# Sigmoid gates rewritten as tanh with VectorE products, and the low weight halves of the input projection moved to VectorE

## The chip, the cores and the metric

The kernel runs on one core of a Trainium2 chip. The metric is the device time of one execution in microseconds; the median of the runs shown stands for the kernel. Five engines work side by side: TensorE (PE in the profile, with its weight loads as PEld), VectorE (DVE), ScalarE (ACT), GpSimd (POOL) and SyncE (SP), which issues the DMAs here. Each engine runs its own instructions strictly in order.

## The reference

Two layers of a hybrid block over 1024 tokens of width 1024, in float32. Cut to what matters here:

```python
h = rmsnorm(x, norm_mix[l])
proj = h @ w_in[l]                      # q | k | v | u | ug | ga | gb : 34 column tiles of 128
a_out = sliding_window_attention(q, k, v, sinks[l])      # window 128, 16 heads, QK norm, rotary
c_out = conformer_conv(u, ug, ...)      # a = u * sigmoid(ug); causal depthwise conv, width 31;
                                        # layernorm; silu; pointwise
merged = sigmoid(ga) * a_out + sigmoid(gb) * c_out
x = x + merged @ w_out[l]
x = x + swiglu(rmsnorm(x, norm_ffn[l]))
```

## The kernel before

Activations lie transposed, channels on the 128 partitions and the 1024 tokens along the row, so a tile is 128x1024. Each matmul of float32 data is made of three matmuls on halves (`mm3`, L236): a value is cut into a high part of type fp32r and a low part, the rest, and high·high, high·low and low·high are added up in PSUM. For the weights, `fetch` (L120) loads one column tile of 128 output channels (`raw`, 128x1024, 512 KB, two buffers) by a DMA on SP, ACT casts it to the high part `wh` (L133, three buffers), and POOL subtracts to get the low part `wl` (L134, two buffers).

A layer is a mix stage (input projection, attention, convolution, merge) and a feed-forward stage. The work of the mix stage is one long loop over 34 projection tiles in the order INPROJ: key and value first, then 30 tiles, then two at the end. `dense` (L257) makes one tile in eight steps of six matmuls and counts a clock step (`tick`, L227) after each. All that goes on beside the projections is hung on this clock: `after(n, fn)` puts `fn` n steps ahead, and what it issues then stands at that place among PE's matmuls. PE's order is written out in this way for the whole program, DVE's for the mix stage only (L755 to the end of the loop). ACT, POOL and SP are ordered by the scheduler of the framework.

Beside the projections run:

- 32 attention units (`unit_s`, L625), one every six steps. Scores S by PE; a copy to SBUF by ACT; mask, maximum `mx` and `nm` by DVE (`top`, 2.2 steps later); the exponentials by ACT (L656), the reciprocal `ri` of their sum by DVE (`norm`, T2 = 3.5 steps after S, L661), scaling by ACT (L663); transposes `pT` by PE (7.5 steps after S); high and low parts `ph` (ACT) and `pl` (DVE, L679); four masks by POOL (L684, L687, tiles `mo`, `ph`, `pl`); the product with the values into `po` by PE (L702), which waits for these masks; and the addition into `A` by DVE (L714).
- Eight query tiles (`queries`, L581), each with a rotation: four DMAs `rot<-q` on SP, two products on POOL (L385, L386), the power that makes the norm (`fq`, L396, POOL), and on DVE a sum (L400) and a low part (L610).
- The convolution (`conv_taps`, L485): per channel tile a first tap (L492) and 30 more (L496) on DVE, one every 1.42 steps, four tiles in a row. Its input `a` is u·sigmoid(ug): ACT's Sigmoid and a product on POOL (L482). After each tile POOL adds it to `lsum` (L502).
- The gates (`gate`, L722): DVE scales the projection (L724), ACT takes Sigmoid (L725). For `ga` a product with A follows on POOL (`mul_a`, L735) and a DMA; `gb` goes to DRAM and is multiplied later (L811).

Reciprocals, taps and low parts thus share one DVE queue whose order is fixed. ACT keeps one set of function tables at a time, and loads another (`ACT_TABLE_LOAD`) wherever Exp and Sigmoid alternate.

Of the kernel before, what the change touches and what calls it, by code (L numbers as in the profile page):

```python
# [12 lines left out]
F32 = mybir.dt.float32  # L13
F32R = mybir.dt.float32r
U32 = mybir.dt.uint32
AF = mybir.ActivationFunctionType
ALU = mybir.AluOpType
# [12 lines left out]
CC = 4  # L30
CW = 31
# [13 lines left out]
V_CWT = 30  # L45
# [7 lines left out]
def trunk(ctx, tc, xT, win, wcv, wout, wgu, wdn, vecs, cosT, sinT, outT):  # L53
    nc = tc.nc
# [61 lines left out]
        wends.append(len(wseq))  # L116
    raws, ready, given = [], [], [0, 0, 0]
    part = [0]

    def fetch(limit=len(wseq)):  # L120
        limit = min(limit, wends[part[0]])
        while given[2] < limit and given[2] <= given[0] + AHEAD + 1:
            src, n = wseq[given[2]]
            raw = wp.tile([P, n], F32, tag="raw", bufs=WRAW, name="raw")
            nc.sync.dma_start(raw, src)
            raws.append(raw)
            given[2] += 1
        while given[1] < given[2] and given[1] <= given[0] + AHEAD:
            n = wseq[given[1]][1]
            raw = raws.pop(0)  # L130
            wh = wp.tile([P, n], F32R, tag="wh", bufs=WHI, name="wh")
            wl = wp.tile([P, n], F32R, tag="wl", bufs=WLO, name="wl")
            nc.scalar.copy(wh, raw)  # L133
            nc.gpsimd.tensor_tensor(out=wl, in0=raw, in1=wh.bitcast(F32), op=ALU.subtract)  # L134
            ready.append((wh, wl))
            given[1] += 1

    def next_w():
        fetch()
        given[0] += 1  # L140
        return ready.pop(0)
# [68 lines left out]
    def at(when, fn):  # L210
        heapq.heappush(events, (when, next(serial), fn))

    def after(n, fn):
        at(clock[0] + n, fn)
# [52 lines left out]
    def t4(name):  # L267
        return tp.tile([P, T], F32, tag="t4", bufs=T4, name=name)
# [52 lines left out]
    for l in range(DEPTH):  # L321
# [32 lines left out]
        ct = mp.tile([P, T], F32, name="ct")  # L354
        st_ = mp.tile([P, T], F32, name="st_")
# [11 lines left out]
        rot = ap_.tile([P, T], F32, name="rot")  # L367
# [9 lines left out]
        def inproj():  # L377
            return dense(xs)

        def rope(src):  # L380
            for h in range(2):
                o = h * HD
                nc.sync.dma_start(rot[o:o + 8], src[o + 8:o + 16])
                nc.sync.dma_start(rot[o + 8:o + 16], src[o:o + 8])
            nc.gpsimd.tensor_tensor(out=src, in0=src, in1=ct, op=ALU.mult)  # L385
            nc.gpsimd.tensor_tensor(out=rot, in0=rot, in1=st_, op=ALU.mult)  # L386

        def headnorm(sq, f):
            pss = ps_o("pssh")
# [78 lines left out]
        held_u = {}  # L468
        avals = {}
# [6 lines left out]
        def conv_g(c, ps):  # L476
            ug = t4("ug")
            nc.vector.tensor_tensor(out=ug, in0=ps, in1=R, op=ALU.mult)
            nc.scalar.activation(ug, ug, AF.Sigmoid)
            a = ap_.tile([P, T + CW - 1], F32, tag="a", bufs=2, name="a")  # L480
            nc.gpsimd.memset(a[:, 0:CW - 1], 0.0)
            nc.gpsimd.tensor_tensor(out=a[:, CW - 1:], in0=held_u.pop(c), in1=ug, op=ALU.mult)  # L482
            after(6, lambda: avals.update({c: a}))

        def conv_taps():  # L485
            for c in range(CC):
                while c not in avals:
                    yield 0
                a = avals.pop(c)
                w0 = V_CWT + c * CW  # L490
                y = ap_.tile([P, T], F32, tag="y", bufs=1, name="y")
                nc.vector.tensor_scalar(out=y, in0=a[:, 0:T], scalar1=V(w0), scalar2=V(V_CB + c),  # L492
                                        op0=ALU.mult, op1=ALU.add)
                yield 1
                for j in range(1, CW):
                    nc.vector.scalar_tensor_tensor(out=y, in0=a[:, j:j + T], scalar=V(w0 + j),  # L496
                                                   in1=y, op0=ALU.mult, op1=ALU.add)
                    if j == CW - 1:
                        if c == 0:
                            nc.scalar.copy(lsum, y)  # L500
                        else:
                            nc.gpsimd.tensor_tensor(out=lsum, in0=lsum, in1=y, op=ALU.add)  # L502
                        nc.sync.dma_start(yd[c], y)
                    yield 1
            while True:
                yield 0

        taps = conv_taps()
        conv_done = [0]

# [70 lines left out]
        def queries(i, ps):  # L581
            q32 = t4("q32")
            nc.scalar.activation(q32, ps, AF.Copy, scale=V(V_GQ))
            sq = t4("sqh")
            nc.scalar.activation(sq, ps, AF.Square)
            rope(q32)
            fq = sm.tile([P, 16], F32, tag="fq", bufs=3, name="fq")
            nfq = sm.tile([P, 16], F32, tag="nfq", bufs=3, name="nfq")
            sr = sm.tile([P, NB, 2], F32, tag="sr", bufs=3, name="sr")
# [33 lines left out]
        Av = {}  # L623
# [98 lines left out]
        def gate(ps):  # L722
            g = t4("g")
            nc.vector.tensor_tensor(out=g, in0=ps, in1=R, op=ALU.mult)  # L724
            nc.scalar.activation(g, g, AF.Sigmoid)  # L725
            return g

        done_o = set()
# [1 line left out]
        def mul_a(i):  # L730
            if (i, 3) not in done_o:
                after(1, lambda: mul_a(i))
                return
            g = gheld.pop(i)
            nc.gpsimd.tensor_tensor(out=g, in0=g, in1=Av.pop(i), op=ALU.mult)  # L735
            nc.sync.dma_start(mA[i], g)


# [14 lines left out]
        after(0 if l else NA, norm_a)  # L753
        dve = ExitStack()
        dve.enter_context(tc.manual_schedule(engines={mybir.EngineType.DVE}))  # L755
        keys(psk)
        tick()
        def project(j):
# [24 lines left out]
        while events:  # L783
            tick()
        assert conv_done[0] == CC * CW
        dve.close()
        att.close()

# [16 lines left out]
        for i in range(8):  # L805
            ga = zp.tile([P, T], F32, tag="ga", bufs=3, name="ga")
            nc.sync.dma_start(ga, mA[i])
            gb = zp.tile([P, T], F32, tag="gb", bufs=3, name="gb")
            nc.sync.dma_start(gb, sB[i])
            ps = dense(zs, True)  # L810
            nc.vector.tensor_tensor(out=gb, in0=ps, in1=gb, op=ALU.mult)  # L811
            nc.vector.tensor_tensor(out=gb, in0=gb, in1=ga, op=ALU.add)
            ms.append(split_plain(gb, f"m{i}"))
        zp_s.close()
# [8 lines left out]
        xacc = [xp.tile([P, T], F32, name=f"xa{e}") for e in range(KD)]  # L823
# [4 lines left out]
        for e in range(KD):  # L828
            nc.sync.dma_start(xacc[e], xT[e] if l == 0 else xnx[e])
            ps = dense(ms, True)  # L830
            if e >= KD - 3:
                ahead(2 * (e - KD + 4))
            nc.vector.tensor_tensor(out=xacc[e], in0=xacc[e], in1=ps, op=ALU.add)
            nc.sync.dma_start(xsp[e], xacc[e])
            tick()
        rgt.close()
# [28 lines left out]
        for e in range(KD):  # L865
            x, g = xacc[e], V(V_GF + e)
            for n in range(2):
# [4 lines left out]
                                               op0=ALU.mult, op1=ALU.subtract)  # L872
# [80 lines left out]
        for f in FORD[:NCL]:  # L953
# [4 lines left out]
            for m in range(2):  # L958
                bs = [bank(), bank()]
                held.append(bs)  # L960
                for kk in range(2):
                    a = next_p()
# [19 lines left out]
        for i, f in enumerate(FORD):  # L982
# [6 lines left out]
            g, u = t4("g"), t4("u")  # L989
# [105 lines left out]
        for n, (name, _, _) in enumerate(DOWN):  # L1095
# [3 lines left out]
            for p in range(NG - fl):  # L1099
                w, a = next_p(), next_p()  # L1100
                for e in range(4):
                    prod(bs[e], w, e, a[0], a[1], go and p == 0, False)
                if 1 <= p < 5 and name in HALVES:
                    up, n = HALVES[name]
# [41 lines left out]
S0 = 16  # L1146
SP = 6.0
TAIL = 2
T1, T2, SCB = 2.2, 3.5, 2
QSP = 7  # L1150
TS = 1.42
LN1 = 7
# [4 lines left out]
QN = 5  # L1157
QSB = 4
WRAW, WHI, WLO, T4 = 2, 3, 2, 4


def _tables():
# [60 lines left out]
```

## Time and profile before

| | us |
|---|---|
| runs shown | 2695.49, 2704.43, 2702.65 |
| median | 2702.65 |
| the profiled execution | 2704.77 |
| its span, first to last instruction | 2703.0 |

| engine | busy us | share of the span |
|---|---|---|
| PE | 2588.6 | 96% |
| DVE | 1843.6 | 68% |
| POOL | 1601.5 | 59% |
| ACT | 1190.6 | 44% |

The page's share of PE counts its pipelined matmuls at their modelled length, so 96% does not say that PE is at its peak; where the granted clock of TensorE is under 1.00, a matmul takes longer and is still busy time. The shares are means over stages that differ: in the mix stage, roughly 105 to 560 us and again 1445 to 1900 us, DVE and POOL work much harder than in the rest. Times are given from the start of the span. In a row of a timeline the columns are start, duration, engine, line, operation, tiles (written <- read), shapes and count, and in brackets how long the engine stood idle just before and what ended that. A row of a group adds up many instructions: busy time and mean duration stand behind the bar.

### The profile page before, as it was taken

The page shows a single profiled execution, that of the slowest core. Times are in us where ns is not written, and L with a number is a line of the kernel's source. Part 1 is how long each engine was busy: PE and PEld are TensorE (multiplying, and loading weights), DVE is VectorE, ACT ScalarE, POOL GpSimd, SP SyncE. Part 2 cuts the span into 40 slices and gives each one's busy share as a digit, 9 for nine tenths or more (in the row PEclk, how much of TensorE's full clock was granted, in tenths as well). Part 3 has the DMA queues.
Part 4 walks back from the last instruction along what each step waited for, and adds up shares of the span by engine and source line. Part 5 has one row for each costly group of instructions (what it writes and reads, how often), then busy time and mean ns, then how long its engine had stood idle before and what let it go on. Part 6 is the DMA issues. An engine that isn't in the chain of part 4 may idle for free.

```text
span 2703.0 us, 33316 instructions
## 1 busy us (share of the span) xinstructions
PE 2588.6 (96%) x11736; PEld 2118.2 (78%) x11736; DVE 1843.6 (68%) x2037; ACT 1190.6 (44%) x2299; POOL 1601.5 (59%) x1028
## 2 busy tenths in 40 slices
PE   7999999999999999999999999989999999999999
PEld 5777777788787888878777777778887788888887
DVE  6689998552567777845637899895616678778344
ACT  2266666742432323344523566668425222223443
POOL 7368776525256767765534777775252677767544
PEclk8999999999999999999999999989999999999999
DMA  3222222475244454476721222234752444455666
GB/s 129 57 66 58 82 80 67 158 271 208 90 164 147 168 179 156 160 269 218 238 67 52 65 88 65 74 93 156 252 203 94 179 168 146 162 179 193 223 223 210
DMA packets 137478, 395.83 MB, mean 146 GB/s; under 512 B 16160, under 2 KB 16416, under 8 KB 137312
## 3 DMA queue, kind: packets, MB, share of 16 engines
q1 hardware_dynamic: 137168, 393.63, 43.3%
q8 instruction: 92, 1.51, 0.2%
q14 instruction: 74, 0.61, 0.1%
q10 hardware_dynamic: 144, 0.09, 0.0%
HBM read 259.17 MB, written 115.34 MB: 139 GB/s over the span
## 4 chain that ended last, share of the span: by engine, by line
PE 64%; DVE 21%; DMA 4%; POOL 4%; issue 3%; ACT 2%; SPq 1%; DVEq 0%; ACTq 0%; POOLq 0%
PE b L850 40%; PE ps L242 20%; DVE y L496 9%; DVE mx L652 1%; DVE sc L648 1%; DVE q L610 1%; DVE acc L295 1%; DVE A L714 1%; DMA qs<-q 1%; PE po L702 1%; POOL q L385 1%; DVE pl L679 1%; DVE g L724 1%; DMA x<-xs 1%; POOL wl L134 1%
## 5 line engine op out<-in xcount | busy, mean ns | idle before, releaser
L151 POOL TENSOR_TENSOR plo<-fraw,phi 128x512 fp32r<-128x512 f32 x290 | 421.4, 1461 | 232.5 <-ACT phi L149 217.4
L134 POOL TENSOR_TENSOR wl<-raw,wh 128x1024 fp32r<-128x1024 f32 (+1 forms) x100 | 241.0, 2411 | 292.2 <-PE ps L242 250.3
L151 POOL TENSOR_TENSOR plo<-fs,phi 128x512 fp32r<-128x512 f32 x160 | 264.7, 1665 | 252.0 <-ACT phi L149 240.4
L496 DVE SCALAR_TENSOR_TENSOR y<-a,vec,y 128x1024 f32<-128x1024 f32 x240 | 402.6, 1678 | 3.6
L149 ACT CAST phi<-fraw 128x512 fp32r<-128x512 f32 x444 | 257.6, 618 | 246.7 <-POOL plo L151 133.6
L242 PE MATMUL ps<-hx,wh 128*128 128x512 f32 x1056 | 350.6, 414 | 7.2 <-ACT hx L283 7.2
L242 PE MATMUL ps<-lx,wh 128*128 128x512 f32 x1056 | 341.0, 405 | 0.8 <-DVE lx L284 0.8
L242 PE MATMUL ps<-hx,wl 128*128 128x512 f32 x1056 | 337.4, 401 | 4.5 <-POOL wl L134 4.5
L149 ACT CAST phi<-fs 128x512 fp32r<-128x512 f32 x160 | 95.4, 620 | 533.9 <-DVE fs L164 520.1
L151 DVE TENSOR_TENSOR plo<-fraw,phi 128x512 fp32r<-128x512 f32 x154 | 129.8, 848 | 191.5 <-ACT phi L149 189.3
L242 PEld LDWEIGHTS ps<-hx,wl 128*128 128x128 f32 x1056 | 206.7, 196 | 50.8 <-POOL wl L134 4.9
L850 PE MATMUL b<-plo,phi 128*128 128x512 f32 x616 | 241.1, 391 | 4.5 <-DVE plo L151 4.2
L242 PEld LDWEIGHTS ps<-lx,wh 128*128 128x128 f32 x1056 | 207.6, 197 | 48.3 <-DVE lx L284 1.5
L850 PE MATMUL b<-phi,plo 128*128 128x512 f32 x616 | 240.4, 390 | 0.0
L850 PE MATMUL b<-phi 128*128 128x512 f32 x616 | 240.4, 390 | 0.0
L242 PEld LDWEIGHTS ps<-hx,wh 128*128 128x128 f32 x1056 | 196.1, 198 | 43.1 <-ACT hx L283 7.2
L133 ACT CAST wh<-raw 128x1024 fp32r<-128x1024 f32 (+1 forms) x100 | 98.1, 981 | 175.7 <-PE ps L242 137.1
L656 ACT ACTIVATE sc<-sc,nm,fq 128x129 f32<-128x129 f32 x256 | 123.8, 486 | 70.4 <-DVE nm L654 69.9
L918 POOL TENSOR_TENSOR g<-g,u 128x512 f32<-128x512 f32 (+1 forms) x84 | 129.3, 1557 | 31.6 <-DVE u L971 25.2
L914 DVE TENSOR_TENSOR g<-g 128x512 f32<-128x512 f32 x88 | 103.9, 1181 | 62.8 <-POOL g L918 42.5
L850 PEld LDWEIGHTS b<-plo,phi 128*128 128x128 f32 x616 | 116.1, 188 | 31.8 <-DVE plo L151 7.8
L850 PEld LDWEIGHTS b<-phi 128*128 128x128 f32 x616 | 116.0, 188 | 24.3
(254 smaller groups left out, 6141.2 us busy)
## 6 DMA issues: line engine op xcount, KB each, us to landing
fraw<-wgu SPq DMA_DIRECT2D x88, 512.0 KB
raw<-win SPq DMA_DIRECT2D x68, 512.0 KB
act<-g SPq DMA_DIRECT2D x44, 512.0 KB
dw<-wdn SPq DMA_DIRECT2D x44, 512.0 KB
td<-g SPq DMA_DIRECT2D x44, 512.0 KB
sd<-dw SPq DMA_DIRECT2D x44, 512.0 KB
fraw<-sd SPq DMA_DIRECT2D x88, 256.0 KB
fraw<-td SPq DMA_DIRECT2D x88, 256.0 KB
```

What stands on the lines that cost most here:

```text
L133: nc.scalar.copy(wh, raw)
L134: nc.gpsimd.tensor_tensor(out=wl, in0=raw, in1=wh.bitcast(F32), op=ALU.subtract)
L149: nc.scalar.copy(hi, src)
L151: (eng or nc.gpsimd).tensor_tensor(out=lo, in0=src, in1=hi.bitcast(F32), op=ALU.subtract)
L242: nc.tensor.matmul(ps[:, sl], a[:, wc], b[:, sl], start=first and j == 0, stop=last and j == 2)
L295: (add or nc.gpsimd).tensor_tensor(out=acc, in0=acc, in1=sq, op=ALU.add)
L385: nc.gpsimd.tensor_tensor(out=src, in0=src, in1=ct, op=ALU.mult)
L496: nc.vector.scalar_tensor_tensor(out=y, in0=a[:, j:j + T], scalar=V(w0 + j), in1=y, op0=ALU.mult, op1=ALU.add)
L656: nc.scalar.activation(sc[:, n], sc[:, n], AF.Exp, bias=nm[:, n:n + 1], scale=fq[:, 4 * j + n:4 * j + n + 1], accum_out=den[:, n:n + 1])
L850: nc.tensor.matmul(ps, w[:, ai * P:(ai + 1) * P], x, start=first and j == 0, stop=last and j == 2, skip_group_check=True)
L914: nc.vector.tensor_tensor(out=o, in0=x, in1=y, op=ALU.subtract)
L918: nc.gpsimd.tensor_tensor(out=g[:, sl], in0=g[:, sl], in1=u[:, sl], op=ALU.mult)
```

## The change

Three things. The sigmoids become tanh: sigmoid(x) = (1 + tanh(x/2))/2. ACT takes Tanh with scale 0.5; the 1 is added in the product, which is now a `scalar_tensor_tensor` on DVE (for `a` 1.5 steps after its gate, for `ga` right behind it, for `gb` in place of the product that was on DVE already); the factor 1/2 goes into the convolution's weights (scaled once per layer by a small DVE instruction) and into the addition behind the output projection. Next, `wl` is made by DVE during the mix loop, two steps (WD) after the point at which `fetch` calls for it; outside it stays on POOL. Last, T2 goes from 3.5 to 4.2, so that the reciprocal stands later in DVE's order. The parameter RD = 0 leaves the rotation on POOL as it was.

```diff
@@ fetch
             nc.scalar.copy(wh, raw)
-            nc.gpsimd.tensor_tensor(out=wl, in0=raw, in1=wh.bitcast(F32), op=ALU.subtract)
+            low(wl, raw, wh)
...
+    def low(wl, raw, wh):
+        if not spaced[0]:
+            nc.gpsimd.tensor_tensor(out=wl, in0=raw, in1=wh.bitcast(F32), op=ALU.subtract)
+            return
+        after(WD, lambda: nc.vector.tensor_tensor(out=wl, in0=raw, in1=wh.bitcast(F32), op=ALU.subtract))
@@ conv_g
-            nc.scalar.activation(ug, ug, AF.Sigmoid)
+            nc.scalar.activation(ug, ug, AF.Tanh, scale=0.5)
...
-            nc.gpsimd.tensor_tensor(out=a[:, CW - 1:], in0=held_u.pop(c), in1=ug, op=ALU.mult)
-            after(6, lambda: avals.update({c: a}))
+
+            def product():
+                nc.vector.scalar_tensor_tensor(out=a[:, CW - 1:], in0=ug, scalar=1.0, in1=held_u.pop(c),
+                                               op0=ALU.add, op1=ALU.mult)
+                avals[c] = a
+            after(1.5, product)
@@ conv_taps
+            nc.vector.tensor_scalar(out=V(V_CWT, CC * CW), in0=V(V_CWT, CC * CW), scalar1=0.5, scalar2=None,
+                                    op0=ALU.mult)
@@ gate
-            nc.scalar.activation(g, g, AF.Sigmoid)
+            nc.scalar.activation(g, g, AF.Tanh, scale=0.5)
@@ mul_a
-            nc.gpsimd.tensor_tensor(out=g, in0=g, in1=Av.pop(i), op=ALU.mult)
+            nc.vector.scalar_tensor_tensor(out=g, in0=g, scalar=1.0, in1=Av.pop(i),
+                                           op0=ALU.add, op1=ALU.mult)
@@ the merge and the output projection
-            nc.vector.tensor_tensor(out=gb, in0=ps, in1=gb, op=ALU.mult)
+            nc.vector.scalar_tensor_tensor(out=gb, in0=gb, scalar=1.0, in1=ps, op0=ALU.add, op1=ALU.mult)
...
-            nc.vector.tensor_tensor(out=xacc[e], in0=xacc[e], in1=ps, op=ALU.add)
+            nc.vector.scalar_tensor_tensor(out=xacc[e], in0=ps, scalar=0.5, in1=xacc[e],
+                                           op0=ALU.mult, op1=ALU.add)
@@ the numbers
-T1, T2, SCB = 2.2, 3.5, 2
+T1, T2, SCB = 2.2, 4.2, 2
...
+WD, RD = 2, 0
```

In the program as built, 60 of the `wl` instructions go from POOL to DVE, 30 in each layer, with 24 products (8 for `a`, 16 for `ga`), and the table loads on ACT go from 73 to 4. PE's order stays the same but for a few small matmuls of the layernorm.

DVE's order around a `ga` gate in the second third of the mix loop, before (`g<-ps,R` scales the projection, `y` are taps, `ri` the reciprocal, `A` the attention sum):

```order
L714 TENSOR_TENSOR A<-po,sh 64x256 x2
L661 RECIPROCAL ri<-den 128x4
L492 TENSOR_SCALAR y<-a,vec_95 128x1024
L496 SCALAR_TENSOR_TENSOR y<-a,vec_95,y 128x1024
L724 TENSOR_TENSOR g<-ps,R 128x1024
L496 SCALAR_TENSOR_TENSOR y<-a,vec_95,y 128x1024
L646 TENSOR_TENSOR sc<-S,mneg 128x2x128
L648 COPY_PREDICATED sc<-mprev,S 128x2x128
L652 TENSOR_REDUCE mx<-sc 128x4
L654 TENSOR_TENSOR nm<-mx,nfq 128x4
L496 SCALAR_TENSOR_TENSOR y<-a,vec_95,y 128x1024
L679 TENSOR_TENSOR pl<-pT,ph 128x512
```

The same place after:

```order
L513 SCALAR_TENSOR_TENSOR y<-a,vec_95,y 128x1024
L678 RECIPROCAL ri<-den 128x4
L513 SCALAR_TENSOR_TENSOR y<-a,vec_95,y 128x1024
L741 TENSOR_TENSOR g<-ps,R 128x1024
L752 SCALAR_TENSOR_TENSOR g<-g,A 128x1024
L513 SCALAR_TENSOR_TENSOR y<-a,vec_95,y 128x1024 x2
L663 TENSOR_TENSOR sc<-S,mneg 128x2x128
L665 COPY_PREDICATED sc<-mprev,S 128x2x128
L669 TENSOR_REDUCE mx<-sc 128x4
L671 TENSOR_TENSOR nm<-mx,nfq 128x4
L696 TENSOR_TENSOR pl<-pT,ph 128x512
L143 TENSOR_TENSOR wl<-raw,wh 128x1024
```

The product `g<-g,A` now stands right behind the scaling, with ACT's tanh between the two; `ri` has one tap more in front of it; and a `wl` has come in behind `pl`.

POOL's order at the rotation of the sixth query tile, before (`q`, `rot` are the rotation, `fq` the power, `mo`, `ph`, `pl` the masks of one attention unit):

```order
L385 TENSOR_TENSOR q_2745<-q_2745,ct 128x1024
L386 TENSOR_TENSOR rot<-rot,st__202 128x1024
L396 TENSOR_TENSOR fq<-ssb,mhalf 128x16
L684 AFFINE_SELECT mo<-ph 128x512
L684 AFFINE_SELECT mo<-pl 128x512
L134 TENSOR_TENSOR wl<-raw,wh 128x1024
L687 AFFINE_SELECT ph<-ph 128x512
L687 AFFINE_SELECT pl<-pl 128x512
L482 TENSOR_TENSOR a<-ur,ug 128x1024
L502 TENSOR_TENSOR lsum<-lsum,y 128x1024
```

After:

```order
L395 TENSOR_TENSOR q_2749<-q_2749,ct 128x1024
L396 TENSOR_TENSOR rot<-rot,st__202 128x1024
L406 TENSOR_TENSOR fq<-ssb,mhalf 128x16
L519 TENSOR_TENSOR lsum<-lsum,y 128x1024
L701 AFFINE_SELECT mo<-ph 128x512
L701 AFFINE_SELECT mo<-pl 128x512
L704 AFFINE_SELECT ph<-ph 128x512
L704 AFFINE_SELECT pl<-pl 128x512
```

`wl` has left the queue between the masks, and `lsum`, which stood behind them, has moved ahead of them. At the seventh query tile the masks follow `fq` with nothing between; at the eighth `lsum` stands between `rot` and `fq`. Before, both had a `wl` between the masks as above.

DVE's order where the convolution begins, before (`kl` is the last low part of the keys, `ssb` belongs to the first query tile):

```order
L441 TENSOR_TENSOR kl_240<-pk,kh_238 128x512
L492 TENSOR_SCALAR y<-a,vec_95 128x1024
L496 SCALAR_TENSOR_TENSOR y<-a,vec_95,y 128x1024 x4
L394 TENSOR_TENSOR ssb<-pssh,e_205 128x16
L496 SCALAR_TENSOR_TENSOR y<-a,vec_95,y 128x1024 x2
```

After:

```order
L451 TENSOR_TENSOR kl_240<-pk,kh_238 128x512
L494 SCALAR_TENSOR_TENSOR a<-ug,ur 128x1024
L509 TENSOR_SCALAR y<-a,vec_95 128x1024
L143 TENSOR_TENSOR wl<-raw,wh 128x1024
L513 SCALAR_TENSOR_TENSOR y<-a,vec_95,y 128x1024 x5
L143 TENSOR_TENSOR wl<-raw,wh 128x1024
L513 SCALAR_TENSOR_TENSOR y<-a,vec_95,y 128x1024 x2
L404 TENSOR_TENSOR ssb<-pssh,e_205 128x16
L513 SCALAR_TENSOR_TENSOR y<-a,vec_95,y 128x1024
```

The product for `a` and two `wl` have come in, and three more taps stand ahead of `ssb`.

## Rows read from the trace of the kernel before

**Rows 1.** The page, part 4: the chain that ended last, by engine and line.
```profile
PE 64%; DVE 21%; DMA 4%; POOL 4%; issue 3%; ACT 2%; SPq 1%; DVEq 0%; ACTq 0%; POOLq 0%
PE b L850 40%; PE ps L242 20%; DVE y L496 9%; DVE mx L652 1%; DVE sc L648 1%; DVE q L610 1%; DVE acc L295 1%; DVE A L714 1%; DMA qs<-q 1%; PE po L702 1%; POOL q L385 1%; DVE pl L679 1%; DVE g L724 1%; DMA x<-xs 1%; POOL wl L134 1%
```

**Rows 2.** Busy time by stretch; after the engines: granted clock, DMA share, GB/s.
```profile
105.00:185.00 80.00, 71.95 (x327) 58.77 (x326) 68.15 (x66) 36.75 (x84) 47.40 (x25) 0.91 0.26 74
185.00:350.00 165.00, 153.69 (x772) 127.07 (x771) 159.15 (x177) 104.10 (x255) 123.07 (x77) 0.96 0.23 67
350.00:500.00 150.00, 136.10 (x676) 113.40 (x676) 124.74 (x148) 99.87 (x236) 104.38 (x71) 0.92 0.29 87
1530.00:1690.00 160.00, 147.78 (x749) 122.17 (x748) 154.28 (x168) 102.62 (x251) 122.16 (x76) 0.97 0.23 69
```

**Rows 3.** The chain of waits inside 185 to 350 us, and inside 350 to 490 us.
```profile
by line: DVE y L496 53.5%; issue 7.5%; DVE mx L652 6.0%; DVE sc L648 5.2%; DVE A L714 5.1%; DVE q L610 4.5%; DVE pl L679 4.1%; DVE g L724 3.0%; DVE q L400 1.6%; POOL lsum L502 1.4%; ACT sc L656 1.2%; DVE y L492 1.2%; DVE ri L661 1.1%; DVE s
...
by line: PE ps L242 18.3%; DVE y L496 13.7%; POOL q L385 7.0%; issue 6.8%; POOL rot L386 5.3%; DMA rot<-q 5.1%; POOL wl L134 5.0%; POOL mo L684 3.9%; POOL pl L687 3.4%; POOL ph L687 3.4%; PE po L702 3.1%; POOL fq L396 3.1%; SPq L383 2.8%; D
```

**Rows 4.** Groups of instructions in 185 to 350 us: DVE's taps, POOL's low parts.
```profile
L496 DVE SCALAR_TENSOR_TENSOR y<-a,vec,y 128x1024 f32<-128x1024 f32 x54 | 94.2, 1744 | 0.8
...
L134 POOL TENSOR_TENSOR wl<-raw,wh 128x1024 fp32r<-128x1024 f32 x10 | 30.1, 3010 | 0.2 <-PE ps L242 0.2
```

**Rows 5.** Durations by line, whole span: ns min/median/max.
```profile
L496 DVE SCALAR_TENSOR_TENSOR y<-a,vec,y x240: 1253/1529/3409, 91.0 to 1817.9; 128x1024 f32<-128x1024 f32 x120
...
L278 DVE TENSOR_TENSOR lm<-gb,hm x16: 1224/1225/1226, 580.4 to 1962.2; 128x1024 fp32r<-128x1024 f32 x16
...
L134 POOL TENSOR_TENSOR wl<-raw,wh x100: 1295/2402/3466, 5.8 to 2022.7; 128x1024 fp32r<-128x1024 f32 x84, 128x512 fp32r<-128x512 f32 x16
```

**Rows 6.** Timeline around 267 us: a low part on POOL and a tap on DVE.
```profile
266.54 2.40 POOL L134 TENSOR_TENSOR wl<-raw,wh 128x1024 fp32r<-128x1024 f32 x1
...
267.05 2.97 DVE L496 SCALAR_TENSOR_TENSOR y<-a,vec,y 128x1024 f32<-128x1024 f32 x1
```

**Rows 7.** Timeline around 230 us: a gate on DVE, then on ACT.
```profile
230.19 1.22 DVE L724 TENSOR_TENSOR g<-ps,R 128x1024 f32<-128x1024 f32 x1
...
231.44 1.06 ACT L725 ACTIVATE g<-g 128x1024 f32<-128x1024 f32 x1 [0.49 <-DVE g L724]
```

**Rows 8.** Timeline 88 to 104 us, DVE: the first taps.
```profile
90.13 0.81 DVE L492 TENSOR_SCALAR y<-a,vec 128x1024 f32<-128x1024 f32 x1 [4.16 <-POOL a L482]
...
102.68 0.17 DVE L394 TENSOR_TENSOR ssb<-pssh,e 128x16 f32<-128x16 f32 x1 [6.45 <-PE pssh L391]
```

**Rows 9.** Who waited for whom, 350 to 500 us: us in total, times, longest.
```profile
PE po L702 <- POOL ph L687: 8.7, 3, 3.0
...
DVE ri L661 <- ACT sc L656: 11.9, 6, 2.6
```

**Rows 10.** Timeline 416 to 432 us: POOL's queue, then PE behind it.
```profile
420.38 2.35 POOL L134 TENSOR_TENSOR wl<-raw,wh 128x1024 fp32r<-128x1024 f32 x1
422.70 1.62 POOL L687 TENSOR_SCALAR_AFFINE_SELECT ph<-ph 128x512 fp32r<-128x512 f32 x1
424.27 1.61 POOL L687 TENSOR_SCALAR_AFFINE_SELECT pl<-pl 128x512 fp32r<-128x512 f32 x1
...
424.37 0.40 PE L702 MATMUL po<-ph,vv 128*128 128x256 f32 x1 [2.65 <-POOL ph L687]
...
427.17 1.05 PE L242 MATMUL ps<-hx,wh 128*128 128x512 f32 x2
```

**Rows 11.** Timeline 478 us, POOL: a sum of the convolution.
```profile
478.68 2.37 POOL L502 TENSOR_TENSOR lsum<-lsum,y 128x1024 f32<-128x1024 f32 x1
```

**Rows 12.** Table loads of ACT, 105 to 500 us, ahead of the exponentials.
```profile
L656 ACT ACT_TABLE_LOAD x13 | 16.7, 1283 | 6.6 <-DVE nm L654 6.4
```

**Rows 13.** SP's queue around 405 us.
```profile
403.66 0.33 SPq L125 DMA_DIRECT2D raw<-win  x1
406.26 0.69 SPq L383 DMA_DIRECT2D rot<-q  x1
```

More of the change, by code (lines that the diff above doesn't have):

```diff
@@ L118, in trunk @@
     part = [0]
+    spaced = [False]
     def fetch(limit=len(wseq)):
@@ L378, in inproj, with rope @@
             return dense(xs)
-        def rope(src):
+        now = lambda n, fn: fn()
+        def rope(src, later=0):
             for h in range(2):
@@ L384, in rope @@
                 nc.sync.dma_start(rot[o + 8:o + 16], src[o:o + 8])
-            nc.gpsimd.tensor_tensor(out=src, in0=src, in1=ct, op=ALU.mult)
-            nc.gpsimd.tensor_tensor(out=rot, in0=rot, in1=st_, op=ALU.mult)
+            eng = nc.vector if later else nc.gpsimd
+            (after if later else now)(later, lambda: eng.tensor_tensor(out=src, in0=src, in1=ct, op=ALU.mult))
+            (after if later else now)(later + 1, lambda: eng.tensor_tensor(out=rot, in0=rot, in1=st_, op=ALU.mult))
         def headnorm(sq, f):
@@ L585, in queries @@
             nc.scalar.activation(sq, ps, AF.Square)
-            rope(q32)
+            rope(q32, RD)
             fq = sm.tile([P, 16], F32, tag="fq", bufs=3, name="fq")
@@ L755, in trunk @@
         dve.enter_context(tc.manual_schedule(engines={mybir.EngineType.DVE}))
+        spaced[0] = True
         keys(psk)
@@ L785, in trunk @@
         assert conv_done[0] == CC * CW
+        spaced[0] = False
         dve.close()
```

## The prediction

> **What bounds the kernel now.** I read the chain of waits first, for which engine ends the program: PE has 64% of it and DVE 21%, but 40% of the span are line L850, the matmuls of the feed-forward stages, which the change doesn't touch; what it touches is the queue in which DVE's taps stand, 9% [rows 1]. So I cut the mix stage of a layer into pieces (105 to 500 us; the second layer repeats it from 1445 us, and its middle piece has DVE busy 154.28 of 160 us [rows 2]). From 185 to 350 us DVE is busy 159.15 of 165 us while PE runs too [rows 2], and the chain inside that piece is on DVE nearly line by line, taps 53.5% [rows 3]: DVE sets the time there. From 350 to 500 us DVE has 25 us of room [rows 2], and the chain is on PE, on taps and, in ten small items, on POOL's queue: rotation, power, low part, masks [rows 3]. There PE stands still at `po` for the masks, 8.7 us in three waits, one at each of the last query tiles [rows 9]; after such a wait a pair of matmuls takes 1.05 us [rows 10], at a granted clock of 0.92 for the piece [rows 2]. ACT is busy 104.10 of 165 us [rows 2] and bounds nothing.
>
> The second thing to see is that DVE and POOL stop each other. A tap alone takes 1253 ns, yet its mean from 185 to 350 us is 1744 [rows 4, 5]: 54 x (1744 - 1253) = 26.5 us of "busy" time in which DVE is held. One case can be watched: a low part on POOL runs from 266.54 to 268.94, a tap starts at 267.05 and takes 2.97 instead of 1.25 us [rows 6]. POOL takes 2.40 us for a low part; the same subtraction with the same types on DVE, `lm`, takes 1.22 [rows 5].
>
> **The change, 105 to 185 us.** DVE is busy 68.15 of 80 us here [rows 2] and stood idle 4.16 us before its first tap and 6.45 us before `ssb` [rows 8]. The order puts three more taps ahead of `ssb`, into that idle time: 3 x 1.25 = 3.8 us that later pieces are spared. The low parts and the product that come in as well use some of it, so I take -3 (0 to -3.8). The convolution's weights, halved once, are a small instruction ahead of the first tap, in the 4.16 us: nothing; without that cover under 0.81 us, which a tensor_scalar on the whole tile takes [rows 8].
>
> **185 to 350 us, where DVE is full.** Added to DVE: ten low parts [rows 4] at 1.22 = 12.2 us, and four products (one `a`, three `ga` gates) at a tap's 1253 ns [rows 5] = 5.0. A new wait comes with each gate: the product stands right behind the scaling, and ACT's tanh needs the time between, 0.03 us to start and 1.06 to run [rows 7], so 3 x 1.1 = 3.3. Queued behind it are taps and the next unit's mask, `mx` and `nm`, for which ACT's exponentials and then PE's transposes wait. If ACT has a copy of scores in front, the wait is longer. Cost: 20.5 us.
>
> Against it stands the held time. How much of the 26.5 us is due to the fourteen instructions that leave POOL, no row says, so I bound it. Low end: share it out by POOL's busy time; the low parts are 30.1 of 123.07 us [rows 2, 4], 24%, hence 6.5 us, 0.65 each; for fourteen 9.1. High end: every one meets a tap as in [rows 6], 2.97 - 1.25 = 1.7 each, 24 in all. I take half of POOL's 2.40 us, 1.2 each, since a tap that comes at any moment of a low part finds half of it left: 16.8 us. Net +3.7, with ends 20.5 - 23.8 = -3.3 and 20.5 - 9.1 = +11.4.
>
> The Trainium skill (Perfetto Trace Analysis, Optimizing Scalar/DVE Operations) speaks against the direction: with DVE saturated, work may be offloaded from it, even to GpSimd. It adds that the two share a read port, so that offloading between them might not help. The tap of 2.97 us [rows 6] agrees with the second half; by the first alone the piece would lose the 20.5 us.
>
> **350 to 500 us, where POOL's queue holds PE.** New work on DVE is some nine low parts and four products, 9 x 1.22 + 4 x 1.25 = 16 us, and fits into its 25 us [rows 2]. In POOL's queue a low part of 2.35 us stands between the masks, and PE restarts after the mask behind it, having waited 2.65 [rows 10]. At the seventh query tile it is gone with nothing in its place: -2.35, and with a shorter stop a shorter stretch of slow matmuls, -1 (0 to -2). At the sixth and eighth, `lsum` moves ahead of the masks (or of `fq`); it takes 2.37 us [rows 11], as much as what left: 0, between -2.35 (if its tap is late and masks were waiting anyway for something else) and +2.4 each.
>
> T2 now puts a tap more in front of `ri`. The 11.9 us that DVE stood waiting for `ri`'s input in this piece [rows 9] go; the price is a later scaling on ACT, and PE's transposes behind it. A tap is 1.25 us, three units near the end of the piece could show it: 0 to +3.8, and I take 0, because PE's three long stops here come from the masks [rows 9]. On SP, a weight load stands ahead of `rot<-q`, issued 2.6 us earlier [rows 13]; its buffer is now freed by DVE's low part, two steps later in the order instead of at POOL's leisure. Nothing as long as that room lasts; past it each us delays the rotation by one. Piece: -3.4.
>
> **The rest.** The 69 table loads that vanish cost ACT 1283 ns each, but they stand in its waits for `nm` (6.4 of 6.6 us idle [rows 12]) and ACT isn't the bound: 0. Merge and output projection: 32 instructions change from 1.22 to at most 1.25 us [rows 5, 7], under 1 us: 0.
>
> Sum of a layer: -3 + 3.7 - 3.4 = -2.7; two layers -5.4. The profiled execution took 2704.77 us, so 2699.4; it stands 2.1 us above the median of the runs shown, and the forecast is **2697**.
>
> **Rivals.** (1) *PE's stops vanish.* If `lsum` is as often late as not, and DVE's relief is at its upper end, a layer gains the whole 8.7 us of stops [rows 9], about 6 us of slow matmuls behind them (an estimate: after each stop some four pairs of matmuls at 1.05 us [rows 10], half of it lost by the clock, 2 us), 3.3 in the full piece and 3.8 at the start: -22, twice -44, **2659**. For it: the three stops have the same cause. Against it: a `lsum` in the same place.
>
> (2) *The shared lock is the only bound.* If DVE and POOL together behave like one engine, every moved low part saves 2.40 - 1.22 and every product 2.40 - 1.25 us: 24 low parts (ten in 165 us, over 395) 28.3, nine products 10.4, per layer -38.7, so **2625**. Against it: DVE's own queue is full at 159.15 of 165, PSUM work included [rows 2], and POOL has 42 us of idle time there.
>
> The skill's rule for this is on the page SBUF — State Buffer, section SBUF: two separate sides: a DVE instruction with two SBUF inputs and a GpSimd instruction exclude each other for the whole instruction. The tap of 2.97 us agrees; that the pair is the bound, no row here shows.
>
> (3) *Slower: the relief is too small.* One mechanism, DVE's queue in its full piece. The cost of 20.5 us is sure, the relief is not. With 8.4 us of relief (0.6 each) the piece costs +12.1, and `ri` behind one tap more adds 1.5 at the transposes; with -3 at the start and nothing gained at the masks that is +10.6 a layer, **2724**. With no relief at all 20.5 + 1.5 - 3 = 19 a layer, 2741. It decides once the relief falls under (20.5 - 6.4) / 14 = 1.0 us for each moved instruction, close below what I took. For it: a low part on DVE is itself one of the instructions that POOL holds, and POOL stays busy with rotations, masks and `lsum`.
>
> (4) *The change doesn't do what it says:* the DMA of the next weights waits for DVE's late low part, and PE for the weights. With three `wh` and two `wl` ahead it would take several us of delay; I count it in (3).
>
> **How the numbers follow.** Forecast 45%, rival 1 18%, rival 2 7%, rival 3 with 4 30%. What a measurement can tell from no change is about 0.3%, 8.1 us. The forecast alone spans 2680 to 2712; of its 45%, 20 fall faster, 20 same, 5 slower. With rivals 1 and 2, faster is 45; rival 3 gives 27 slower and 3 same: faster 0.45, same 0.23, slower 0.32. The range reaches to rivals 1 and 3, 2655 to 2726; outside lie rival 2 and the outer parts of 1 and 3, some 20%.
>
> **What would show it.** In the profile after: low parts on DVE at a mean near 1.22 (well above says that POOL holds them); the taps' mean from 185 to 350 us down from 1744 to about 1430 (16.8 us over 54), and still 1650 if rival 3 holds; DVE's wait for ACT's tanh, 1.1 us each; PE's waits at `po` for `ph` two per layer instead of three, none under rival 1; DVE's wait at `ri` gone, and no new wait of PE for scaled scores; ACT some 88 us less busy in all (69 x 1.283) with no gain from it; rotation loads on SP no later. The prediction is wrong at its root if the stretch from 185 to 350 us is no longer led by DVE, or if the time moved lies outside the mix stages.

## The result, and the profile after

| | before | after |
|---|---|---|
| median of the runs, us | 2700.11 (2695.49 to 2704.43) | 2678.14 (2675.03 to 2681.57) |
| after / before | | 0.9924, 95% interval 0.9909 to 0.9940 |
| the profiled execution, us | 2704.77 | 2675.03 |

The change makes the kernel 0.76% faster, 20 to 22 us. The forecast was 2697, so the sign and the range held; the gain forecast, 5.4 us, is a quarter of the one measured. Each trace below shows one execution. That of the kernel before took 4.7 us more than the median, and its mean granted clock, 0.975, is below that of the other executions on record (0.977 to 0.985), so a few us of any difference between traces can be chance.

The page of after, its span and its part 1:

```profile
span 2673.3 us, 33211 instructions
...
PE 2571.2 (96%) x11736; PEld 2099.2 (79%) x11736; DVE 1864.7 (70%) x2123; ACT 1100.6 (41%) x2230; POOL 1397.3 (52%) x944
```

POOL lost 204 us of work and ACT 90; DVE's busy time rose by 21 us only, although it took over 60 low parts and 24 products. Busy time by stretch after, to be laid beside [rows 2]:

```profile
105.00:185.00 80.00, 75.93 (x383) 62.62 (x382) 76.06 (x90) 42.59 (x110) 33.50 (x26) 1.00 0.27 76
185.00:350.00 165.00, 150.54 (x757) 124.70 (x756) 152.23 (x181) 87.67 (x235) 84.83 (x62) 0.95 0.24 70
350.00:500.00 150.00, 141.19 (x702) 115.46 (x701) 128.87 (x162) 89.69 (x233) 78.30 (x58) 0.97 0.34 108
```

From 105 to 185 us DVE is now busy 76 of 80 us (68 before), from 185 to 350 us 152 of 165 (159 before), and the granted clock of TensorE from 105 to 185 us rose from 0.91 to 1.00. The groups from 185 to 350 us after, beside [rows 4]: taps, low parts on DVE, products of the gates.

```profile
L513 DVE SCALAR_TENSOR_TENSOR y<-a,vec,y 128x1024 f32<-128x1024 f32 x53 | 81.8, 1543 | 0.7
L143 DVE TENSOR_TENSOR wl<-raw,wh 128x1024 fp32r<-128x1024 f32 x10 | 13.7, 1370 | 0.0
...
L752 DVE SCALAR_TENSOR_TENSOR g<-g,A 128x1024 f32<-128x1024 f32 x3 | 3.7, 1225 | 4.0 <-ACT g L742 4.0
```

A tap fell from 1744 to 1543 ns, a low part on DVE takes 1370 (alone it would be 1.22 us), and DVE stands 4.0 us before three products, waiting for tanh. The waits from 350 to 500 us after, beside [rows 9], of PE and of DVE:

```profile
PE pT L689 <- ACT sc L680: 4.7, 5, 2.1
...
PE po L719 <- POOL ph L704: 1.1, 2, 0.6
```

```profile
DVE g L752 <- ACT g L742: 3.4, 3, 1.1
...
DVE ri L678 <- ACT sc L673: 1.3, 3, 0.5
```

The 8.7 us that PE stood at `po` are 1.1, the 11.9 us that DVE stood at `ri` are 1.3, and new in this window are PE's waits at the transposes `pT` for scaled scores.

**The whole stage as one sum.** To compare kernels I cut at the same work: from the 192nd to the 1440th projection matmul on PE, which is the mix stage of the first layer from the first gates on. The busy time of that stretch, before and then after (columns as in [rows 2]):

```profile
84.40:519.00 434.60, 401.34 (x1968) 332.33 (x1966) 375.65 (x415) 263.43 (x617) 290.85 (x183) 0.94 0.28 83
```

```profile
81.30:506.20 424.90, 396.76 (x1983) 327.15 (x1981) 378.75 (x456) 228.94 (x594) 205.05 (x149) 0.97 0.28 86
```

DVE's busy time is the same within 3.1 us; what shrank is its idle time, 434.6 - 375.7 = 58.9 to 424.9 - 378.8 = 46.1 us. That is the first hint that the moved work paid for itself and that the gain came from a wait. The time moved lies in the mix stages: the 1440th matmul starts 12.8 us earlier (519.0 to 506.2 us), and the same work of the second layer takes 16.8 us less (the last row of the table of pieces below), of 29.7 us between the two profiled executions.

### The profile page after: what moved, and what is told of

The parts are those of the page before. It is cut to its first block, busy times and chain, and to the rows that moved or that the text cites. A ratio compares the mean times of both kernels' runs of the same rounds, so it can differ in the third digit from the quotient of the medians.

```text
span 2673.3 us, 33211 instructions
## 1 busy us (share of the span) xinstructions
PE 2571.2 (96%) x11736; PEld 2099.2 (79%) x11736; DVE 1864.7 (70%) x2123; ACT 1100.6 (41%) x2230; POOL 1397.3 (52%) x944
## 3 DMA queue, kind: packets, MB, share of 16 engines
q1 hardware_dynamic: 137168, 393.63, 43.6%
## 5 line engine op out<-in xcount | busy, mean ns | idle before, releaser
L513 DVE SCALAR_TENSOR_TENSOR y<-a,vec,y 128x1024 f32<-128x1024 f32 x240 | 369.2, 1538 | 3.1
L249 PE MATMUL ps<-hx,wh 128*128 128x512 f32 x1056 | 344.5, 408 | 7.4 <-ACT hx L290 7.4
L249 PE MATMUL ps<-lx,wh 128*128 128x512 f32 x1056 | 333.9, 397 | 0.8 <-DVE lx L291 0.8
L701 POOL TENSOR_SCALAR_AFFINE_SELECT mo<-ph 128x512 fp32r<-128x512 f32 x64 | 63.3, 989 | 235.3 <-ACT ph L691 235.3
L141 POOL TENSOR_TENSOR wl<-raw,wh 128x1024 fp32r<-128x1024 f32 (+1 forms) x40 | 80.2, 2006 | 191.8 <-PE ps L249 174.7
L704 POOL TENSOR_SCALAR_AFFINE_SELECT ph<-ph 128x512 fp32r<-128x512 f32 x64 | 78.0, 1218 | 163.6 <-DVE pl L696 163.6
```

Of the source, the lines that this page charges most:

```text
L249: nc.tensor.matmul(ps[:, sl], a[:, wc], b[:, sl], start=first and j == 0, stop=last and j == 2)
L701: nc.gpsimd.affine_select(out=mo, in_=src.bitcast(F32), pattern=[[0, 4], [1, P]], compare_op=ALU.is_ge, fill=0.0, base=0, channel_multipli ...
L704: nc.gpsimd.affine_select(out=src, in_=src.bitcast(F32), pattern=[[0, 4], [-1, P]], compare_op=ALU.is_gt, fill=0.0, base=0, channel_multip ...
```

## The experiments

The change has three parts that can be put in one by one: the low parts on DVE (L), the gates by tanh with products on DVE (G), and T2 = 4.2 (T). First I asked where L gains.

**e1_wl_pool**, the change without L:

```diff
-        spaced[0] = True
+        spaced[0] = False
```

> The changed kernel with its low weight parts back on POOL for the whole program; tanh, the products on DVE and T2 = 4.2 stay. Theory S (the gain of 22 us is the low parts' leaving POOL, and most of it lies in the first 185 us of each mix stage, where they stood ahead of the rotation and held the sums and low parts on DVE): all of that gain is gone, and the 12 products with their waits for tanh stay on DVE, so 2698 to 2712, with the waits of PE for the first query loads back. Rival G (the gates do it: products off POOL, fewer table loads, the later reciprocal): the gain stays, 2676 to 2684.

Measured 2681.76, ratio 0.9935 (0.9920 to 0.9950). Theory S falls: without the low parts 18 of the 22 us are still gained.

**e2_wl_only**, L alone, put into the kernel before:

```diff
-            nc.gpsimd.tensor_tensor(out=wl, in0=raw, in1=wh.bitcast(F32), op=ALU.subtract)
+            low(wl, raw, wh)
```

> The kernel before with one part of the change: the low weight parts on DVE, two steps later, during the mix loop. Sigmoid, the products on POOL and T2 = 3.5 stay as before. Theory S: 2672 to 2684, as fast as the whole change or a little faster. Rival G: 2694 to 2705, no gain. By the prediction's own terms (start -3, middle piece 12.2 of cost against 12 of relief, -3.4 at the masks) it would be about 2690.

Measured 2677.09, ratio 0.9918 (0.9903 to 0.9933). So rival G falls as well, and L alone is 13 us faster than the prediction's own terms make it. L alone and G with T each give the gain of the whole or most of it, and they do not add up.

**e6_wl_early** and **e7_wl_late**, L only in the first, or only in the later part of the loop:

```diff
             project(j)
+            if idx == 8:
+                spaced[0] = False
```

> The changed kernel with the low parts on DVE only for the keys and the first nine tiles of the mix loop (up to about 185 us in the first layer), on POOL after that. Theory S: the gain of the start (13 and 16 us in the two layers by the times at which PE reaches the same matmul) stays: 2675 to 2686, with the masks' waits at the last query tiles back. By the prediction's sum, in which the start is worth 3 us a layer, 2692 to 2700.

> The opposite: low parts on POOL for the keys and the first nine tiles, on DVE from the tenth on. Theory S: 2696 to 2706, the gain of the start is gone and what is left (the middle piece's loss of about 4 a layer against 4 to 6 at the end) is near nothing. By the prediction's sum 2697 to 2703; if the gain comes from DVE's relief in its full piece, under 2688.

Measured 2666.59, ratio 0.9878 (0.9861 to 0.9894), and 2688.85, ratio 0.9963 (0.9950 to 0.9976). Low parts on DVE up to 185 us gain 15 us (2681.8 to 2666.6); later in the loop they cost 12 (2666.6 to 2678.1) or 7 (2681.8 to 2688.9). So e6_wl_early is faster than either expectation had it, and e7_wl_late lies between its two. Of the 15 us, 9.5 lie ahead of the 192nd projection matmul: it starts at 85.6 us in e1_wl_pool and at 80.9 in e6_wl_early, and in the second layer 37.0 and 32.2 us after the 96th. One cause there can be seen at the keys: before, a low part on POOL runs while the sum `k` takes 2.55 us, and PE waits for that sum (DVE, POOL and PE around 65 us, before):

```profile
64.42 2.41 POOL L134 TENSOR_TENSOR wl<-raw,wh 128x1024 fp32r<-128x1024 f32 x1 [2.15 <-PE ps L242]
65.37 2.55 DVE L400 TENSOR_TENSOR k<-k,rot 128x1024 f32<-128x1024 f32 x1
...
68.06 0.63 PE L424 MATMUL ptk<-ident,k 128*128 128x128 f32 x4 [1.15 <-DVE k L400]
```

After, with nothing on POOL, the same sum takes 1.22 us and PE does not wait:

```profile
64.93 1.22 DVE L410 TENSOR_TENSOR k<-k,rot 128x1024 f32<-128x1024 f32 x1
...
66.31 0.61 PE L434 MATMUL ptk<-ident,k 128*128 128x128 f32 x4
```

**q_act.** At the second query tile the framework had also changed SP's order: `qs<-q` stood behind a weight load, and no longer does. This run moves only these loads:

```diff
-                        nc.sync.dma_start(q[o], q32[r])
+                        (nc.scalar if i == 1 else nc.sync).dma_start(q[o], q32[r])
```

> The kernel before with one edit: the two loads of the low query halves of the second query tile (qs<-q, one tile of eight in each layer) are issued from ACT's queue instead of SP's; the orders of PE, DVE and POOL stay the same, row for row. Before, these loads stand on SP behind a weight load that waits for its buffer until POOL has made a low part; in the changed kernel, with the gates alone and with the low parts alone they stand ahead of it. Theory Q (this place in SP's order is the common cause of the 11 us that PE gains between its 288th and 576th projection matmul in each layer, with either half of the change): the stop of 2.8 us at the scores and the slow matmuls behind it go, 2680 to 2688. Rival H (POOL's shorter queue or DVE's relief does it, and SP's order is a side effect): 2696 to 2704.

Measured 2693.42, ratio 0.9977 (0.9968 to 0.9987): between the two. Before, SP issues the loads after the weight load and a store (SP's queue), and PE stands at the scores (PE):

```profile
164.92 0.33 SPq L125 DMA_DIRECT2D raw<-win  x1
165.35 0.38 SPq L770 DMA_DIRECT2D sB<-g  x1
165.82 1.86 SPq L616 DMA_DIRECT2D qs<-q  x2
```

```profile
171.76 0.30 PE L636 MATMUL S<-kh,qs 128*128 128x128 f32 x1 [2.22 <-DMA qs<-q]
```

In q_act these scores run without a wait, and 5.4 us are gained, 2.7 a layer, so the place in SP's order does cost time in the kernel before, though little. How the gain arises is not shown: in the trace of q_act, the slowest of its twelve executions (2697.66 us), all of PE's waits in the first layer's stretch add up to 33 us, as before.

**e4_sigmoid**, the change with Sigmoid instead of tanh:

```diff
-            nc.scalar.activation(g, g, AF.Tanh, scale=0.5)
+            nc.scalar.activation(g, g, AF.Sigmoid)
```

> The changed kernel with Sigmoid on ACT in place of tanh (and plain products on DVE, no factors of 1/2): all of the change but the table loads, of which some 70 come back. The prediction priced them at nothing, since they stand in ACT's waits for the maximum: 2674 to 2682. Rival: ACT's 1.28 us in front of exponentials or behind the gate's scaling reaches DVE's product or PE, 2684 to 2700.

Measured 2693.62, ratio 0.9974 (0.9960 to 0.9987); without tanh 15 us of the gain are lost (13.5 by the two ratios). The products of the gates and of `a`, 80.5 to 519 us:

```profile
L748 DVE TENSOR_TENSOR g<-g,A 128x1024 f32<-128x1024 f32 x6 | 7.3, 1225 | 12.7 <-ACT g L738 12.7
...
L494 DVE TENSOR_TENSOR a<-ug,ur 128x1024 f32<-128x1024 f32 x4 | 5.2, 1291 | 4.2 <-ACT ug L489 4.2
```

With a table load in front of the sigmoid DVE waits 12.7 + 4.2 us a layer at its products; in the change it is 7.3 + 0.4. With DVE's queue right behind them the loads cost something. Whether they cost nothing as long as POOL made the products is not shown, since no run takes them out of the kernel before.

**e5_mul_later**, the product of `ga` 1.5 steps after its gate:

```diff
             g = gheld.pop(i)
-            nc.vector.scalar_tensor_tensor(out=g, in0=g, scalar=1.0, in1=Av.pop(i),
+            after(1.5, lambda: prod_a(i))
```

> The changed kernel with the product of a ga gate 1.5 steps later, so that DVE does taps while ACT takes the tanh. The prediction priced the wait at 3 x 1.1 us in DVE's full piece: 3.3 us a layer back, 2669 to 2675. If what waits there is hidden because DVE would have waited elsewhere, 2676 to 2681.

Measured 2672.15, ratio 0.9903 (0.9890 to 0.9916): the wait for tanh falls from 7.3 to 1.7 us a layer, and 6 us are gained, as priced.

**e3_t2_35**, the change without T:

```diff
-T1, T2, SCB = 2.2, 4.2, 2
+T1, T2, SCB = 2.2, 3.5, 2
```

> The changed kernel with T2 back at 3.5. In the changed kernel PE waits five or six times a layer for the scaled scores (0.7 to 2.1 us each at pT). If the later reciprocal causes this, those waits go and 2664 to 2672 is reached; if the reciprocal now makes DVE wait for ACT's exponentials, as in the kernel before (11.9 us in the last piece), 2680 to 2690; if neither, 2675 to 2681.

Measured 2698.69, ratio 1.0000 (0.9991 to 1.0009). All of the gain is gone, worse than any expectation. So L and G together give nothing without T, and the one number that the prediction priced at 0, taken away last, takes the whole gain with it. This holds for this order only: L alone, without T, gave as much as the whole change.

**t2_before, t2_wl, gates_35**: T alone, L with T, G alone, which completes the table of the three parts.

```diff
-T1, T2, SCB = 2.2, 3.5, 2
+T1, T2, SCB = 2.2, 4.2, 2
```

> The kernel before with T2 = 4.2 alone. In the kernel before DVE stands 17.7 us a layer at the reciprocal waiting for ACT's exponentials, and the prediction priced their removal at 0 (0 to +3.8 a layer lost at PE's transposes). Theory D (DVE sets the pace in more of the mix stage than its full piece, so that its waits at the reciprocal count): 2680 to 2692. The prediction's price: 2697 to 2706.

> Low parts on DVE and T2 = 4.2; the gates stay Sigmoid with products on POOL. The low parts alone gave 2677. Theory D: DVE still waits 14 us a layer at the reciprocal there, so 2658 to 2670. If the later reciprocal pays only together with the products on DVE (where T2 = 3.5 took away the whole gain), 2674 to 2682.

> Tanh and the products on DVE, with low parts on POOL and T2 = 3.5: the gates alone. With T2 = 4.2 they gave 2682. Theory D: the products add about 15 us and the wait for tanh about 7 us of DVE time a layer, and DVE is late at the reciprocal as before, so the gain goes: 2692 to 2706. If the gates themselves carry the gain: 2680 to 2688.

Measured 2683.91, ratio 0.9936 (0.9918 to 0.9953); 2665.14, ratio 0.9869 (0.9855 to 0.9884); 2694.14, ratio 0.9978 (0.9967 to 0.9989). All three are where theory D put them. The medians (the kernel before lay between 2698.8 and 2701.0 beside the different sets of runs):

| | T2 = 3.5 | T2 = 4.2 | T gains |
|---|---|---|---|
| neither | 2701.0 | 2683.9 | 17.1 |
| low parts | 2677.1 | 2665.1 | 12.0 |
| gates | 2694.1 | 2681.8 | 12.3 |
| both | 2698.7 | 2678.1 | 20.6 |

T gains 12 to 21 us in every row of this table. L gains 24 us alone, 19 beside T, 4 beside G and T, and loses 5 beside G; G gains 7 alone and 2 beside T, and loses 22 beside L and 13 beside L and T. The three parts do not add up, and T is the only one that gains in every combination. The same stretch of the first layer in t2_before and in e3_t2_35 (busy time, columns as above):

```profile
83.10:508.50 425.40, 395.63 (x1968) 324.66 (x1966) 375.89 (x415) 261.95 (x617) 284.27 (x183) 0.97 0.28 85
```

```profile
80.70:518.00 437.30, 396.57 (x1983) 329.39 (x1982) 384.29 (x456) 228.44 (x595) 199.44 (x149) 0.95 0.28 84
```

In t2_before DVE's work is the same as before, 375.9 us, its idle time falls by 9.4 and the stretch by 9.2: DVE's idle time is the gain. Who waited over this stretch, before, in t2_before, in e3_t2_35 and with L alone (e2_wl_only):

```profile
DVE ri L661 <- ACT sc L656: 17.7, 10, 2.6
...
PE po L702 <- POOL ph L687: 9.2, 4, 3.0
```

```profile
DVE ri L661 <- ACT sc L656: 8.0, 5, 2.6
...
PE pT L672 <- ACT sc L663: 13.4, 12, 2.1
...
PE po L702 <- POOL ph L687: 1.4, 2, 0.9
```

```profile
PE po L719 <- DVE ssb L404: 20.7, 6, 5.2
```

```profile
PE po L709 <- DVE ssb L401: 24.2, 6, 4.9
```

T takes 9.7 us from DVE's wait at `ri`. PE's long stops at `po` turn into more and shorter ones at `pT`; all its waits in the stretch shrink only from 33 to 30 us. The rest is 5.7 us less of busy time for the same matmuls, at a granted clock of 0.97 instead of 0.94 (the two rows of busy time, before and t2_before). In the change T shows in another place: PE's busy time is the same in e3_t2_35 and in the change (396.6 and 396.8 us), and its idle time is 40.7 and 28.1 us. In e3_t2_35 PE stands 20.7 us at `po` for DVE's `ssb`, but this wait alone does not make a kernel slow: with L alone it is 24.2 us, and the time is 2677. How DVE's wait at `ri` arises, at the eighth query tile before, on ACT and on DVE:

```profile
455.26 0.48 ACT L656 ACTIVATE sc<-sc,nm,fq 128x129 f32<-128x129 f32 x1
455.74 1.09 ACT L583 ACTIVATE q<-ps,vec 128x1024 f32<-128x1024 f32 x1
456.74 1.01 ACT L585 ACTIVATE sqh<-ps 128x1024 f32<-128x1024 f32 x1
457.64 0.49 ACT L656 ACTIVATE sc<-sc,nm,fq 128x129 f32<-128x129 f32 x1
...
455.25 0.84 DVE L714 TENSOR_TENSOR A<-po,sh 64x256 f32<-64x256 f32 x2
458.73 0.18 DVE L661 RECIPROCAL ri<-den 128x4 f32<-128x4 f32 x1 [2.63 <-ACT sc L656]
```

A copy and a square of the query (L583, L585), 2.1 us together, stand among ACT's exponentials, and DVE waits 2.63 us. In t2_before the same place on DVE:

```profile
448.42 0.85 DVE L714 TENSOR_TENSOR A<-po,sh 64x256 f32<-64x256 f32 x2
449.30 1.64 DVE L496 SCALAR_TENSOR_TENSOR y<-a,vec,y 128x1024 f32<-128x1024 f32 x1
450.85 0.17 DVE L661 RECIPROCAL ri<-den 128x4 f32<-128x4 f32 x1
```

A tap fills the time, and the reciprocal starts at once.

**early_later**, e6_wl_early and e5_mul_later together, meant to beat both kernels:

> A version meant to beat both: the changed kernel with low parts on DVE only up to the ninth tile of the loop (2666.6 alone) and the ga products 1.5 steps later (2672.2 alone). If the two gains, 11.5 and 6 us, add up, since one frees DVE of ten instructions a layer in its full piece and the other of its waits for tanh: 2658 to 2664. If they pay for the same idle time: 2664 to 2669.

Measured 2666.57, ratio 0.9875 (0.9859 to 0.9892), the same as e6_wl_early: the two gains do not add up, as expected if they pay for the same idle time. It is 12 us faster than the change. With less code t2_wl, the change without its gates, is 13 us faster.

The pieces of the first layer by kernel, cut at the 192nd, 576th, 960th and 1440th projection matmul (starts of these matmuls in the traces, us), and the second layer from its 96th to its 1440th:

```
piece          before  L      T      L+T    G+T    L+G    all
192 to 576     124.3   116.8  122.0  116.7  113.5  120.8  119.1
576 to 960     138.2   140.3  139.3  137.8  142.1  145.1  137.8
960 to 1440    172.1   167.1  164.0  163.2  167.2  171.4  168.0
second layer   471.4   455.0  461.1  449.6  462.9  468.9  454.6
```

## Why the prediction was right in sign and short in size

**The failed step is T2.** The prediction wrote: "The 11.9 us that DVE stood waiting for `ri`'s input in this piece [rows 9] go", and then took 0 with bounds of 0 to +3.8, "because PE's three long stops here come from the masks". No gain was allowed at all. The runs put T at -12 to -21 us, -20.6 in this change; with that in place of 0 the forecast of 2697 becomes 2676, against 2678 measured. Two readings led there. DVE's room of 25 us from 350 to 500 us was taken for slack, though for 11.9 us of it DVE stood at `ri` with work queued behind. And PE's stops at `po` were put down to their last releaser, POOL's masks behind a low part: in t2_before POOL's order at the sixth and seventh query tile is the same, low part included, and the stops for `ph` there, 3.0 and 2.65 us before, are 0.9 and 0.5 us. Nor does T pay only in this piece: by the table of pieces it gains 8.1 us in the last piece when it comes alone, and in the change 1.7, 7.3 and 3.4 us in the three. That the sign held owes something to luck: the terms that were to bring the gain, L and G, brought none together, and the one that brought it stood at 0.

**The moved work, priced near zero, was near zero, for L and G together.** The prediction's sum, with T2 at 0, gives -5.4 us for L and G; e3_t2_35 measures 0, within 2.4. Each of them alone gains, 24 and 7 us, which the sum does not have. The relief of 1.2 us for each instruction that leaves POOL holds over the stage. In the stretch above 36 instructions came to DVE:

```profile
L143 DVE TENSOR_TENSOR wl<-raw,wh 128x1024 fp32r<-128x1024 f32 x26 | 34.0, 1306 | 0.0
...
L752 DVE SCALAR_TENSOR_TENSOR g<-g,A 128x1024 f32<-128x1024 f32 x6 | 7.4, 1226 | 7.3 <-ACT g L742 7.3
...
L494 DVE SCALAR_TENSOR_TENSOR a<-ug,ur 128x1024 f32<-128x1024 f32 x4 | 5.3, 1330 | 0.4 <-ACT ug L489 0.4
```

They took 34.0 + 7.4 + 5.3 = 46.7 us of their own, and DVE's busy time rose by 3.1, so 43.6 us of held time went, 1.2 each (1.1 at the 1.22 and 1.25 us of the prediction). Taps alone gave less in the full piece than expected (a mean of 1543 instead of some 1430 ns); the query's low part and `nm` gave most of the rest, from 185 to 350 us before and then after:

```profile
L610 DVE TENSOR_TENSOR q<-q,qhi 128x1024 fp32r<-128x1024 f32 x3 | 7.6, 2536 | 0.0
L654 DVE TENSOR_TENSOR nm<-mx,nfq 128x4 f32<-128x4 f32 x13 | 7.0, 535 | 0.4
```

```profile
L627 DVE TENSOR_TENSOR q<-q,qhi 128x1024 fp32r<-128x1024 f32 x3 | 3.6, 1207 | 0.2 <-ACT qhi L624 0.2
L671 DVE TENSOR_TENSOR nm<-mx,nfq 128x4 f32<-128x4 f32 x12 | 3.1, 262 | 0.4
```

**The start was mis-sized.** It was priced at -3 a layer. L early gains 15 us in all, against e1_wl_pool, and 9.5 of them lie ahead of 105 us and its counterpart in the second layer, where the prediction's pieces had not begun. The taps moved into idle time are there, but the prediction did not look at what POOL's low parts held on the way to PE, such as the sum `k` at 65 us, nor at SP's order at the second query tile (2.7 us a layer by q_act).

**The full piece was near for the whole, not for its parts.** It was priced at +3.7. From the 576th to the 960th matmul (208.7 to 346.9 us before) all together it is -0.4 us in the first layer and +4.0 in the second, and L+G without T +6.9 and +7.9. Low parts on DVE after the ninth tile cost 12 us in the program.

**Waits and tables.** The wait for tanh was priced at 1.1 us each; it was 7.3 us for six, and e5_mul_later got 6 us back. The table loads were priced at 0 because they stood in ACT's waits; no run tests this in the kernel before. Beside products on DVE they cost some 15 us (e4_sigmoid), so tanh is needed once the products have moved.

**The expected signs.** The wait for tanh, fewer stops at `po` for `ph`, next to no wait at `ri`, ACT 90 us less, rotation loads no later (POOL's wait for them falls from 16.0 to 6.9 us in the stretch): seen. Low parts on DVE took 1.31 us on average over the stretch, near 1.22 but held now and then, and the taps' mean fell two thirds as far as expected. ACT's 90 us "with no gain from it": not so beside products on DVE. "No new wait of PE for scaled scores": not so, PE's waits at `pT` in the stretch rise from 2.4 to 12.4 us, and this is what T costs. Whether DVE still leads the time from 185 to 350 us is not shown; it is busy 152 of 165 us there. Rival 1 (2659) was right that the stops for `ph` go, but all of PE's waits in the stretch fall only from 33 to 28 us; rival 3 needed a relief under 1.0 us each, and it was 1.1 to 1.2. The Trainium skill (Perfetto Trace Analysis, Optimizing Scalar/DVE Operations) says of offloading between DVE and GpSimd that it might not help. The ratio of 1.0000 in e3_t2_35 agrees with that; 0.9918 in e2_wl_only, with the low parts alone, does not.

What stays open: through which of the waits DVE's earlier arrival reaches PE's clock, and why L and G gain singly at the start (7.5 us and, with T, 10.8 us in the first piece) and not together. That the second finds no idle time left on DVE would fit, but no run takes either apart. G also holds a shift that no run separates: a tile's taps no longer wait six steps behind its gate, so the convolution ends earlier in the loop, its last tap starting behind the 1272nd projection matmul instead of the 1314th.

## What to carry to other kernels

Idle time of an in-order engine is slack only if nothing queued behind the waiting instruction is needed soon; count it at every instruction that waits, over the whole stage, before calling the engine unhurried. When a change bundles work that moves with a number that shifts an order, price the number alone: here it was the cheapest part, and without it the bundle gave nothing. Price every part alone and beside the others too, since here the low parts alone gave as much as the bundle. Then look for the version that keeps what pays and drops the rest, as 2665 us (low parts and T2, no new gates) shows.

## What the runs showed of the hardware

A low part or product of 128x1024 that left POOL, where it took 2.4 us or more, gave DVE 1.2 us of held time back on average, about as much as it took on DVE (46.7 us for 36): DVE's busy time rose by 3.1 us over the stretch. By the same count it was 1.5 us each with the low parts alone (e2_wl_only), 0.9 with the products alone (gates_35) and 1.1 without T (e3_t2_35). And a table load of 1.28 us on ACT in front of a gate's sigmoid cost DVE about 0.9 us of waiting each time (5.4 us more at six products) once DVE's queue stood behind it.
